# Key rope projection moved from two split-precision units to sixteen plain fp32 matmuls on four column tiles, with other work moved

## The chip, the cores and the metric

The kernel runs on one NeuronCore of one Trainium2 chip. The metric is the device time of one execution in microseconds (us), lower is better. TensorE (PE) does the matmuls, VectorE (DVE) and ScalarE (ACT) the elementwise work, GpSimd (POOL) and SyncE (SP) small jobs and the issue of DMAs.

## The reference, cut to what matters

One layer of a hybrid attention block, all in fp32, over 256 prompt tokens and 64 sample tokens (T = 320 token columns together). What the change touches is the MLA branch:

```python
h = rmsnorm(x, norm_pre[l])
proj = jnp.einsum('bsd,de->bse', h, w_in[l])          # D = 2048 in, 15392 out
a_qkv, b_qkv, c_qkv, d_in, gate_in, merge_in = jnp.split(proj, SPLIT_POINTS, axis=-1)
q_down, kv_down, k_rope_in = jnp.split(d_in, (Q_LORA, Q_LORA + KV_LORA), axis=-1)   # 384, 128, 32
q_mla = jnp.einsum('bsr,re->bse', rmsnorm(q_down, mla_q_norm[l]), mla_w_q_up[l])
ckv = rmsnorm(kv_down, mla_kv_norm[l])
k_rope = rope(k_rope_in, pos)                          # 32 columns
kv = jnp.einsum('bkr,re->bke', ckv_all, mla_w_kv_up[l])
```

The other parts are three attention branches (A stick-breaking, B banded, C differential), gates, branch and merge projections, the output projection and a last norm.

## The kernel before, in words

**Units.** The weights stream through the chip once, cut into units of at most 128x1024 elements. Each unit is loaded by SP (`emit_load`, L156, four buffers `raw`), split into a rounded high half on ACT (L193, `whi`) and the low rest on DVE (L194, `wlo`), and multiplied on PE. An fp32 product is made of three fast matmuls (`mm3`, L197 to L200: high x high, high x low, low x high), each 128x128 weights by 320 columns. A usual unit holds 256 output columns for four slices of the input, 24 matmuls; four such units (j = 0 to 3) make one group, which adds up in one of two PSUM buffers, `pm0` and `pm1`, that groups take in turn (`new_pm`, L102). After its last unit the group's `post` reads the buffer out; the buffer can be written again only when all of these reads are done. The input x is split once in the same way (`xhi`, `xlo`; first eight units).

**Slots.** The main loop (L1243 to L1267) runs one slot per unit i. In slot i it emits, in this order: the load for unit i+3, the split of unit i+3, a step of the background work (`run_background`, L283), the unit's matmuls, and its `post`. `whi` and `wlo` have four buffers, so the split of unit i+3 can start only when PE has finished unit i-1. Every engine runs its instructions in the order in which they were emitted (the schedule is written by hand).

**Order of the units.** Before: 0 to 7 the latent projections of branch D (`d_units`, L902; 512 columns, in two `pm` buffers); 8 and 9 the key rope (`krope_units`, L788); 10 to 13 the first A query; 14 `kv_unit(0)` (L826); 15 to 18 A key; 19 `kv_unit(1)`; 20 `q_unit(0)` (L855); 21 to 24 A value; 25 `q_unit(1)`; 26 to 29 a gate; 30 `q_unit(2)`; then groups of four to the end of the first phase, then merges and branches, then the output projection.

**Key rope.** Its 32 columns and a copy of them with the halves swapped are one weight of 64 columns. The split puts the high and the low half side by side (`pack`, L180 to L186), so one 128-column weight serves both, and two matmuls per input slice (L799, L800) give the product: 32 matmuls in all. `post` adds the two halves, scales and rotates.

**Work around it.** `x_rms` (L1198) sums the squares of x on PE, ahead of unit 7; the squares come from a chain of adds on DVE (`x_sum`, L1196). `x_rbc` (L1208), ahead of unit 8, spreads the norm over all partitions. The post of units 0 to 7 runs in slot 8 and starts `kv_norm` and `q_norm` (L746, L773) as background work: `q_norm` first steps in slot 9, waits 3 slots, sums on PE in slot 12, waits 4 slots, and in slot 16 makes three transposes on PE (L585), three scalings on DVE (L783), the high half `qh` on ACT (L785) and the low half `ql` on DVE (L786), which the `q_unit`s multiply by.

**kv_unit and q_unit.** `kv_unit` takes a `pm` buffer for the keys and two of the four small `att` PSUM buffers for the values (18 matmuls), and reads the `pm` buffer out with two copies on DVE (L847) and two on ACT (L848), the values with L843, L849 and L850, and copies the rope keys in with L852. `q_unit(0)` has 18 matmuls and six DVE operations behind them (L875 to L880).

**Attention in the background.** `pair` (L248) steps the attention of two head pairs at a time. Scores of the first go into the PSUM buffer that the running group does not use (`spare_pm`, L106). A `yield n, True` is a place where both wait until such a buffer may be taken: `spare_ok` (L245) allows it in the second and third unit of a group (j = 1 and 2).

**Start.** SP loads the first slice of x, ACT's queue the first weights. Meanwhile PE multiplies a tile of ones seven times (`spin`, L130).

Of the kernel before, what the change touches and what calls it, by code (L numbers as in the profile page):

```python
# [29 lines left out]
NCP = 128  # L30
# [30 lines left out]
def hybrid_streaming_kernel(ctx, tc, ins, outs):  # L61
# [48 lines left out]
    def att():  # L110
        return psa.tile([128, 512], F32, name="att", tag="att", bufs=4)
# [6 lines left out]
    ident = cpool.tile([128, NCP], F32, name="ident")  # L118
# [3 lines left out]
    def load_x(a, b):  # L122
        nc.sync.dma_start(xf[:, a:b, :], ins["x_t"][:, a:b, :])
# [6 lines left out]
    spin = att()  # L130
    for _ in range(7):
        nc.tensor.matmul(spin[:, 0:128], ones, ones, start=True, stop=True)
# [7 lines left out]
    def rb(n, i=0, rows=slice(0, 128), cols=slice(0, T)):  # L140
        w = cols.stop - cols.start
        r = rbc[rows, i:i + 1, cols]
        return r if n == 1 else r.to_broadcast([rows.stop - rows.start, n, w])
# [15 lines left out]
    def load_part(q, u, k0, k1, c0=0, c1=None):  # L159
# [5 lines left out]
        q.dma_start(raw[:, k0:k1, c0:c1], src[:, k0:k1, c0:c1])  # L165
# [10 lines left out]
    def emit_split(u):  # L176
        n = u["kn"] * u["cols"]
        hi = wpool.tile([128, 1024], F32R, name="whi", tag="whi", bufs=NHL)
        raw = u["raw"][:, :n]
        if u.get("pack"):  # L180
            hl = hi.rearrange("p (k o c) -> p k o c", o=2, c=u["cols"])
            raw = raw.rearrange("p (k c) -> p k c", c=u["cols"])
            nc.scalar.activation(hl[:, :, 0, :], raw, AF.Copy)
            nc.vector.tensor_tensor(hl[:, :, 1, :], raw, hl[:, :, 0, :].bitcast(F32), op=OP.subtract)
            u["hi"] = hi
            return  # L186
# [58 lines left out]
    def spare_ok():  # L245
        return slot[0] >= len(units) or units[slot[0]].get("left", 0) > 0

    def pair(*gens):  # L248


        live = [dict(gen=g, due=0, bar=None) for g in gens]
        while live:
            go = True
            while go:
# [10 lines left out]
                if live and all(e["bar"] and e["due"] <= slot[0] for e in live):  # L265
                    if live[0]["bar"][1] and not spare_ok():
# [201 lines left out]
    def attn_softmax(kind, n, hf, p, q, k, v, bias_heads=None):  # L468
# [13 lines left out]
        yield 0, True  # L482
# [17 lines left out]
        yield 0, False  # L500
# [19 lines left out]
        if kind != "C":  # L520
            for c, (a, b) in enumerate(BLK):
                nc.vector.tensor_scalar(z[:, a:b], z[:, a:b], rs[:, c:c + 1], None, op0=OP.mult)
            yield 2, True
            zt = transposes_pt(z, p)
            yield 2, False
# [12 lines left out]
        yield 3, False  # L538
# [9 lines left out]
        yield 2, False  # L548
# [10 lines left out]
        yield 2, False  # L559
# [28 lines left out]
    def attn_stick(n, hf, p, q, k, v):  # L588
# [4 lines left out]
        yield 0, True  # L593
# [11 lines left out]
        yield 0, False  # L605
# [52 lines left out]
        yield 2, False  # L658
# [73 lines left out]
    def post_d1(ps):  # L732
# [4 lines left out]
        scaled(M["kvd"][:, 0:1, :], ps[:, 1:2, :T], 1)  # L737
        scaled(M["qd"][:, 2:3, :], ps[:, 0:1, :T], 1)
# [49 lines left out]
    def krope_units():  # L788
        box = {}

        def mk(j):
            def mm(u):
                if j == 0:
                    box["ps"] = att()[:, :T]
                h = u["hi"].rearrange("p (k c) -> p k c", c=128)
                ps = box["ps"]
                for kk in range(8):
                    k = 8 * j + kk
                    nc.tensor.matmul(ps, h[:, kk, :], xhi[:, k, :], start=k == 0, stop=False)  # L799
                    nc.tensor.matmul(ps, h[:, kk, :], xlo[:, k, :], start=False, stop=k == 15)  # L800
            return mm

        def post():

            p1, ps, ce, kr = R["p1"], box["ps"], R["ce"], M["kr"]
            ka = p1.tile([96, 2, T], F32, name="ka", tag="t0", bufs=2)
            nc.scalar.activation(ka[0:64, 0, :], ps[64:128, :], AF.Copy)
            nc.vector.tensor_tensor(ka[0:64, 0, :], ka[0:64, 0, :], ps[0:64, :], op=OP.add)
            nc.vector.tensor_tensor(ka[0:64, 0, :], ka[0:64, 0, :], rbc[0:64, 0, :], op=OP.mult)
            nc.vector.tensor_tensor(kr[64:96, 0:T], ka[0:32, 0, :], ce[0:32, C_CS:C_CS + T], op=OP.mult)  # L810
            nc.vector.tensor_tensor(ka[64:96, 1, :], ka[32:64, 0, :], ce[32:64, C_CS:C_CS + T], op=OP.mult)
            nc.vector.tensor_tensor(kr[64:96, 0:T], kr[64:96, 0:T], ka[64:96, 1, :], op=OP.add)
            kz = p1.tile([128, 2, 448], F32, name="kz", tag="t2", bufs=2)
            M["kz"] = kz
            nc.gpsimd.memset(kz[64:128], 0.0)
            for j in range(2):
                for o in range(2):
                    a = 64 + 32 * o + 16 * j
                    nc.gpsimd.dma_start(kz[a:a + 16, j, :], kr[64 + 16 * o:80 + 16 * o, :])
            defer(lambda: nc.sync.dma_start(O["o_krope_t"], kr[64:96, 0:T]))  # L820

        for j in range(2):
            units.append(dict(src=w_kr[j * 1024:(j + 1) * 1024, :], kn=8, cols=64, mm=mk(j),
                              post=post if j == 1 else None, pack=True))
# [77 lines left out]
    def d_units():  # L902
# [4 lines left out]
        def mk(j):  # L907
            def mm(u):
                if j == 0:
                    box.extend(new_pm() for _ in range(2))  # L910
                h, l = (u[n].rearrange("p (k c) -> p k c", c=512) for n in ("hi", "lo"))
                for kk in range(2):
                    k = 2 * j + kk
                    wx = ((h, xhi), (h, xlo), (l, xhi))
# [293 lines left out]
    def x_rbc():  # L1208
        tp = att()
        for t, n in TN:  # L1210
            nc.tensor.transpose(tp[:, t * 128:t * 128 + n], rstat[:n, 2 * t:2 * t + 1].to_broadcast([n, 128]), ident[:n, :n])
        nc.scalar.activation(rbc[:, 0, :], tp[:, :T], AF.Copy)
        nc.vector.tensor_scalar(rbc[:, 1, :], tp[:, :T], 0.125, None, op0=OP.mult)
# [10 lines left out]
             6: [lambda: x_sum(0, 2, 2), lambda: x_sum(0, 1, 1)]}  # L1224
    late = {7: x_rms, 8: x_rbc}
# [17 lines left out]
    for i, u in enumerate(units):  # L1243
# [83 lines left out]
```

## Time and profile before

| what | value |
|---|---|
| median of 3 runs | 1178.18 us (1177.75 to 1178.98) |
| the profiled execution's own time | 1178.78 us |
| its span, first to last instruction | 1176.9 us |
| PE busy | 1166.2 us (99%) |
| DVE, ACT, POOL busy | 611.0, 507.2, 62.2 us (52%, 43%, 5%) |
| DMA | 182.94 MB, mean 155 GB/s |
| mean granted TensorE clock | 0.999 |

Busy time is that in which an engine works on at least one instruction. Matmuls overlap in the pipeline, so one that is shown with 0.31 us can follow the one ahead of it by 0.147 us; the distance between starts is what counts. A plain fp32 matmul appears as two records, one for each of its two passes.

### The profile page before, as it was taken

How to read it: one execution, taken by the hardware profiler on the slowest of the kernel's cores; microseconds unless marked ns; L12 is line 12 of the kernel's file. 1: busy time of each engine (PE TensorE's matmuls, PEld its weight loads, DVE VectorE, ACT ScalarE, POOL GpSimd, SP SyncE). 2: the span in 40 equal slices, each digit the busy share in tenths (PEclk: the TensorE clock that was granted, in tenths of full speed). 3: DMA queues.
4: the chain of work that ended last, by engine and by line, in shares of the span. 5: the costliest groups of instructions: out<-in, count | busy, mean ns of one | idle time of the engine just before them, and what ended most of it. 6: DMA issues, size and time to landing. Idle time of an engine off the chain costs nothing.

```text
span 1176.9 us, 19581 instructions
## 1 busy us (share of the span) xinstructions
PE 1166.2 (99%) x8135; PEld 1154.3 (98%) x8135; DVE 611.0 (52%) x853; ACT 507.2 (43%) x732; POOL 62.2 (5%) x124
## 2 busy tenths in 40 slices
PE   9999999999999999999999999999999999999997
PEld 9999999999999999999999999999999999999997
DVE  7583547455664547547445454454444454454444
ACT  8444664347445546535333333333333333334442
POOL 0312000002022100000000000000000000020000
PEclk9999999999999999999999999999999999999999
DMA  8866435545455544455554555555555555565442
GB/s 271 245 193 186 131 113 162 155 145 149 148 163 142 160 143 137 126 160 145 148 157 141 154 145 151 155 150 144 158 147 144 161 144 148 157 201 180 144 125 90
DMA packets 173449, 182.94 MB, mean 155 GB/s; under 512 B 9197, under 2 KB 167265, under 8 KB 172945
## 3 DMA queue, kind: packets, MB, share of 16 engines
q1 hardware_dynamic: 169488, 173.20, 50.1%
q0 software_dynamic: 2656, 5.32, 1.7%
q10 hardware_dynamic: 1216, 3.18, 0.9%
q8 instruction: 64, 1.05, 0.4%
q14 instruction: 25, 0.20, 0.1%
HBM read 174.79 MB, written 9.39 MB: 156 GB/s over the span
## 4 chain that ended last, share of the span: by engine, by line
PE 96%; ACT 1%; DMA 1%; DVE 1%; issue 0%; SPq 0%; DVEq 0%
PE pm L198 30%; PE pm L200 29%; PE pm L199 29%; PE att L411 1%; DMA raw<-in_w_in 1%; PE pm L1116 0%; PE pm L1118 0%; PE pm L1117 0%; ACT xhi L1185 0%; ACT whi L171 0%; PE pm L921 0%; PE att L648 0%; PE sp L498 0%; PE att L1081 0%; DVE xsq L1196 0%
## 5 line engine op out<-in xcount | busy, mean ns | idle before, releaser
L194 DVE TENSOR_TENSOR wlo<-raw,whi 128x1024 fp32r<-128x1024 f32 (+1 forms) x301 | 366.3, 1222 | 456.3 <-ACT whi L193 454.6
L198 PE MATMUL pm<-xhi,whi 128*128 128x320 f32 x1856 | 577.1, 311 | 0.0
L200 PE MATMUL pm<-xhi,wlo 128*128 128x320 f32 x1856 | 573.5, 309 | 0.0
L199 PE MATMUL pm<-xlo,whi 128*128 128x320 f32 x1856 | 573.5, 309 | 0.0
L193 ACT ACTIVATE whi<-raw 128x1024 fp32r<-128x1024 f32 (+1 forms) x301 | 315.1, 1052 | 411.3 <-PE pm L199 329.7
L198 PEld LDWEIGHTS pm<-xhi,whi 128*128 128x128 f32 x1856 | 348.4, 188 | 1.8 <-PE att L200 0.6
L199 PEld LDWEIGHTS pm<-xlo,whi 128*128 128x128 f32 x1856 | 348.5, 188 | 0.2
L200 PEld LDWEIGHTS pm<-xhi,wlo 128*128 128x128 f32 x1856 | 348.4, 188 | 0.0
L198 PE MATMUL pm<-ghi,whi 128*128 128x320 f32 x256 | 79.1, 309 | 0.0
L199 PE MATMUL pm<-glo,whi 128*128 128x320 f32 x256 | 79.1, 309 | 0.0
L200 PE MATMUL pm<-ghi,wlo 128*128 128x320 f32 x256 | 79.1, 309 | 0.0
L970 ACT ACTIVATE sg<-sg 128x640 f32<-128x640 f32 x32 | 23.7, 741 | 111.3 <-DVE sg L147 111.3
L198 PE MATMUL pm<-yhi,whi 128*128 128x320 f32 x224 | 69.7, 311 | 0.0
L199 PE MATMUL pm<-ylo,whi 128*128 128x320 f32 x224 | 69.2, 309 | 0.0
L200 PE MATMUL pm<-yhi,wlo 128*128 128x320 f32 x224 | 69.2, 309 | 0.0
L147 DVE TENSOR_TENSOR sg<-pm,rbc 128x640 f32<-128x640 f32 x40 | 33.0, 824 | 44.6 <-PE pm L200 44.6
L198 PEld LDWEIGHTS pm<-ghi,whi 128*128 128x128 f32 x256 | 48.0, 188 | 0.0
L199 PEld LDWEIGHTS pm<-glo,whi 128*128 128x128 f32 x256 | 48.0, 188 | 0.0
L200 PEld LDWEIGHTS pm<-ghi,wlo 128*128 128x128 f32 x256 | 48.0, 188 | 0.0
L199 PEld LDWEIGHTS pm<-ylo,whi 128*128 128x128 f32 x224 | 42.1, 188 | 0.0
L198 PEld LDWEIGHTS pm<-yhi,whi 128*128 128x128 f32 x224 | 42.1, 188 | 0.0
L200 PEld LDWEIGHTS pm<-yhi,wlo 128*128 128x128 f32 x224 | 42.0, 188 | 0.0
(330 smaller groups left out, 892.8 us busy)
## 6 DMA issues: line engine op xcount, KB each, us to landing
raw<-in_w_in SPq DMA_DIRECT2D x237, 512.0 KB, 3.8
raw<-in_w_branch SPq DMA_DIRECT2D x32, 512.0 KB, 3.6
raw<-in_w_out SPq DMA_DIRECT2D x32, 512.0 KB, 3.7
xrp<-in_x_prompt SPq DMA_DIRECT2D x1, 2048.0 KB, 7.7
out_xp<-ytp SPq DMA_DIRECT2D x8, 256.0 KB, 2.1
xf<-in_x_t SPq DMA_DIRECT2D x5, 321.0 KB, 7.5
scr<-in_bb ACTq DMA_DIRECT2D x1, 1536.0 KB, 8.9
bp<-scr POOLq DMA_DIRECT2D x12, 128.0 KB, 2.4
```

The lines of the kernel that those rows point to most:

```text
L147: nc.vector.tensor_tensor(out, ps, rb(n, i, rows, cols), op=OP.mult)
L193: nc.scalar.activation(h, raw, AF.Copy)
L194: nc.vector.tensor_tensor(l, raw, h.bitcast(F32), op=OP.subtract)
L198: nc.tensor.matmul(out, wh, xh, start=first, stop=False)
L199: nc.tensor.matmul(out, wh, xl, start=False, stop=False)
L200: nc.tensor.matmul(out, wl, xh, start=False, stop=last)
L411: nc.tensor.matmul(o[64 * j:64 * j + 64, a:b], v[:, blk, vc + 64 * j:vc + 64 * j + 64], z[j][blk], start=first, stop=not first)
L970: nc.scalar.activation(s, s, AF.Sigmoid)
```

## The change

- The key rope's two units go. Its weight (128 x 16 x 32) is loaded once by SP into its own tile `wkr` behind the identity, and multiplied by `norm_pre` on DVE in slot 6 (`kr_scale`). Sixteen plain fp32 matmuls of 32 output columns each, from the unsplit x (`krope_mm`, behind unit 7), add up on four column tiles of the array: slice k on tile k mod 4. In slot 9 ACT copies the result to SBUF, and in slot 10 one fp32 matmul with a constant of 64 columns (`sel`) adds the four tiles and makes the swapped copy; the rotation follows as before (`krope`).
- `x_rms` is emitted inside unit 7, between its two input slices, instead of ahead of it. Its PSUM tile serves `x_rbc` too.
- The D units use one `pm` buffer and two `att` buffers, instead of two `pm` buffers.
- Order of the units after: 0 to 7 D; 8 to 11 A query; 12 to 15 A key; 16 `kv_unit(0)`; 17 `kv_unit(1)`; 18 `q_unit(0)`; 19 to 22 A value; 23 `q_unit(1)`; 24 to 27 a gate; 28 `q_unit(2)`. The slots of `q_norm` stay 9, 12 and 16.
- The places at which scores take the spare buffer allow only j = 2 now; those for transposes still j = 1 and 2.
- The first loads of x and of the weights are halved by partitions over SP's and ACT's queues; `spin` runs eight times, in a spare `pm` buffer.

```diff
-    def spare_ok():
-        return slot[0] >= len(units) or units[slot[0]].get("left", 0) > 0
+    def spare_ok(most):
+        return slot[0] >= len(units) or 0 < units[slot[0]].get("left", 0) <= most
...
-    spin = att()
-    for _ in range(7):
+    spin = spare_pm()[:, 0]
+    for _ in range(8):
...
-        yield 0, True
+        yield 0, 1
...
-            yield 2, True
+            yield 2, 2
...
+    def krope_mm():
+
+        M["krp"] = att()
+        for k in range(KC):
+            c = slice(32 * (k % 4), 32 * (k % 4) + 32)
+            nc.tensor.matmul(M["krp"][c, :T], wkr[:, k, :], xf[:, k, :T], start=k < 4, stop=k >= KC - 4)
+
+    def krope():
+        p1, ce, kr = R["p1"], R["ce"], M["kr"]
+        ka = p1.tile([128, 2, T], F32, name="ka", tag="t0", bufs=2)
+        nc.scalar.activation(ka[:, 0, :], M["krp"][:, :T], AF.Copy)
+        yield 1
+
+        ps = att()[:, :T]
+        nc.tensor.matmul(ps[0:64], sel, ka[:, 0, :], start=True, stop=True)
+        nc.vector.tensor_tensor(ka[0:64, 1, :], ps[0:64], rbc[0:64, 0, :], op=OP.mult)
...
                 if j == 0:
-                    box.extend(new_pm() for _ in range(2))
+                    box.append(new_pm())
+                    box.append([att(), att()])
...
+                    if k == KC - 1:
+                        x_rms()
...
+                if j == 7:
+                    krope_mm()
...
     d_units()
-    krope_units()
...
     aq()
+    ak()
     kv_unit(0)
-    ak()
     kv_unit(1)
     q_unit(0)
...
-    load_part(nc.scalar, units[0], 0, 1, 0, 256)
-    load_x(0, 1)
-    load_part(nc.scalar, units[0], 0, 1, 256, 512)
+    for q, r in ((nc.sync, slice(0, 64)), (nc.scalar, slice(64, 128))):
+        load_x(0, 1, q, r)
+        load_part(q, units[0], 0, 1, 0, 256, r)
+    load_part(nc.sync, units[0], 0, 1, 256, 512)
...
+    def kr_scale():
+        nc.vector.tensor_tensor(wkr, wkr, xf[:, :, T:T + 1].to_broadcast([128, KC, 32]), op=OP.mult)
...
-             6: [lambda: x_sum(0, 2, 2), lambda: x_sum(0, 1, 1)]}
-    late = {7: x_rms, 8: x_rbc}
+             6: [lambda: x_sum(0, 2, 2), lambda: x_sum(0, 1, 1), kr_scale]}
+    late = {8: x_rbc}
...
-                nc.sync.dma_start(ident, ins["cp"])
+                nc.sync.dma_start(cp, ins["cp"])
+                nc.sync.dma_start(wkr, ins["w_kr"])
                 nc.sync.dma_start(nrm, ins["nrm"])
```

## Rows read from the trace of the kernel before

**Rows 1.** The page: busy time by engine; the chain by engine.

```profile
PE 1166.2 (99%) x8135; PEld 1154.3 (98%) x8135; DVE 611.0 (52%) x853; ACT 507.2 (43%) x732; POOL 62.2 (5%) x124
...
PE 96%; ACT 1%; DMA 1%; DVE 1%; issue 0%; SPq 0%; DVEq 0%
```

**Rows 2.** Waits of PE, whole span: us in total, times, longest.

```profile
PE sp L498 <- DVE sg L147: 1.6, 1, 1.6
PE att L1202 <- DVE xsq L1196: 1.1, 1, 1.1
...
```

**Rows 3.** Timeline, PE, 30 to 42 us: start, us, what, idle before.

```profile
30.45 0.31 PE L921 MATMUL pm<-xhi,wlo 128*128 128x320 f32 x1
31.84 0.81 PE L1202 MATMUL att<-ones,xsq 128*128 128x2 f32 x6 [1.08 <-DVE xsq L1196]
32.58 0.41 PE L921 MATMUL pm<-xhi,whi 128*128 128x320 f32 x1
...
36.71 0.42 PE L799 MATMUL att<-xhi,whi 128*128 128x320 f32 x1
...
41.50 0.72 PE L576 MATMUL att<-ones,kvd 128*128 128x2 f32 x6
```

**Rows 4.** Timeline, DVE, 29 to 32 us.

```profile
29.83 0.69 DVE L184 TENSOR_TENSOR whi<-raw,whi 128x512 fp32r<-128x512 f32 x1
30.43 1.35 DVE L1196 TENSOR_TENSOR xsq<-xsq 128x640 f32<-128x640 f32 x2
```

**Rows 5.** Timeline, DVE, second attention of C: 450 to 458 us.

```profile
453.26 0.82 DVE L147 TENSOR_TENSOR sg<-pm,rbc 128x640 f32<-128x640 f32 x1
...
457.57 0.35 DVE L397 CUSTOM_DVE_ANT_0 z<-sp,bs 128x192 f32<-128x192 f32 x1
```

**Rows 6.** Timeline, PE, 0 to 8 us.

```profile
1.04 3.35 PE L132 MATMUL att<-ones 128*128 128x128 f32 x14 [1.04 <-POOL ones L129]
4.76 0.90 PE L921 MATMUL pm<-xhi,whi 128*128 128x320 f32 x2 [0.36 <-ACT whi L171]
```

**Rows 7.** Chain that ended last, its longest pieces: start, us, what.

```profile
148.28 1.92 PE att L411 x32
...
440.94 1.08 PE att L567 x4
```

**Rows 8.** L411 in all: duration ns min/median/max, first and last start, forms.

```profile
L411 PE MATMUL att<-zt,v x128: 219/247/431, 148.2 to 395.4; 128*64 128x64 f32 x64, 128*64 128x256 f32 x32, 128*64 128x128 f32 x32
```

**Rows 9.** Timeline, DVE, slot 16: 67 to 73 us.

```profile
68.07 1.45 DVE L783 SCALAR_TENSOR_TENSOR qd<-qd,smallp,att 128x320 f32<-128x320 f32 x3
70.59 1.16 DVE L786 TENSOR_TENSOR ql<-qd,qh 128x960 fp32r<-128x960 f32 x1 [1.07 <-ACT qh L785]
71.66 0.95 DVE L194 TENSOR_TENSOR wlo<-raw,whi 128x768 fp32r<-128x768 f32 x1
```

**Rows 10.** Timeline, PE, transposes of slot 16; starts of units 19, 20, 21.

```profile
64.33 0.49 PE L585 MATMUL att<-ident,rs 128*128 128x128 f32 x3
64.58 0.39 PE L198 MATMUL pm<-xhi,whi 128*128 128x320 f32 x1
...
75.22 0.36 PE L198 MATMUL pm<-ch,whi 128*128 128x448 f32 x1
...
77.86 0.31 PE L198 MATMUL pm<-qh,whi 128*128 128x320 f32 x1
...
80.49 0.31 PE L198 MATMUL pm<-xhi,whi 128*128 128x320 f32 x1
```

**Rows 11.** Timeline, DVE, slot 19: 75 to 82 us.

```profile
75.42 0.82 DVE L147 TENSOR_TENSOR k<-pm,rbc 128x640 f32<-128x640 f32 x1 [1.30 <-PE pm L200]
76.42 1.22 DVE L194 TENSOR_TENSOR wlo<-raw,whi 128x1024 fp32r<-128x1024 f32 x1 [0.17 <-ACT whi L193]
77.56 0.61 DVE L847 COPY kd<-pm 64x448 f32<-64x448 f32 x1
78.78 0.62 DVE L847 COPY kd<-pm 64x448 f32<-64x448 f32 x1 [0.61 <-ACT kd L848]
...
81.26 1.23 DVE L194 TENSOR_TENSOR wlo<-raw,whi 128x1024 fp32r<-128x1024 f32 x1
```

**Rows 12.** Timeline, ACT, slot 19: the last read of the buffer.

```profile
79.43 0.54 ACT L848 ACTIVATE kd<-pm 64x448 f32<-64x448 f32 x1 [0.68 <-DVE kd L847]
```

More of the change, by code (lines that the diff above doesn't have):

```diff
@@ L28 @@
 LAM_INIT = 0.8 - 0.6 * math.exp(-0.0)
-NCP = 128
+NCP = 192
 C_TRI, C_MD, C_MS, C_CS, C_OH = 0, 128, 384, 512, 832
@@ L37, in make_consts @@
     cp[:, 0:128] = np.eye(128)
+    r = np.arange(128) % 32
+    cp[np.arange(128), 128 + r] = cp[np.arange(128), 160 + (r + 16) % 32] = 1.0
     ce = np.zeros((128, NCE), np.float32)
@@ L117, in hybrid_streaming_kernel, with load_x @@
     xsq = ppool.tile([128, KC, T], F32, name="xsq")
-    ident = cpool.tile([128, NCP], F32, name="ident")
+    cp = cpool.tile([128, NCP], F32, name="cp")
+    ident, sel = cp[:, 0:128], cp[:, 128:192]
+    wkr = ppool.tile([128, KC, 32], F32, name="wkr")
     nrm = cpool.tile([128, 24], F32, name="nrm")
     npost = nrm[:, 0:16]
-    def load_x(a, b):
-        nc.sync.dma_start(xf[:, a:b, :], ins["x_t"][:, a:b, :])
+    def load_x(a, b, q=nc.sync, r=slice(0, 128)):
+        q.dma_start(xf[r, a:b, :], ins["x_t"][r, a:b, :])
     eps = cpool.tile([128, 1], F32, name="eps")
@@ L142, in rb @@
         r = rbc[rows, i:i + 1, cols]
-        return r if n == 1 else r.to_broadcast([rows.stop - rows.start, n, w])
+        return r[:, 0] if n == 1 else r.to_broadcast([rows.stop - rows.start, n, w])
     def scaled(out, ps, n, i=0, rows=slice(0, 128), cols=slice(0, T)):
@@ L157, in emit_load, with load_part @@
         load_part(nc.sync, u, 0, u["kn"])
-    def load_part(q, u, k0, k1, c0=0, c1=None):
+    def load_part(q, u, k0, k1, c0=0, c1=None, r=slice(0, 128)):
         kn, c = u["kn"], u["cols"]
@@ L164, in load_part @@
         src = u["src"].rearrange("(k p) c -> p k c", p=128)
-        q.dma_start(raw[:, k0:k1, c0:c1], src[:, k0:k1, c0:c1])
+        q.dma_start(raw[r, k0:k1, c0:c1], src[r, k0:k1, c0:c1])
     def hi_part(u, a, b):
@@ L179, in emit_split @@
         raw = u["raw"][:, :n]
[L180 to L186, printed above, removed]
         lo = wpool.tile([128, 1024], F32R, name="wlo", tag="wlo", bufs=NHL)
@@ L265, in pair @@
                 if live and all(e["bar"] and e["due"] <= slot[0] for e in live):
-                    if live[0]["bar"][1] and not spare_ok():
+                    if live[0]["bar"][1] and not spare_ok(live[0]["bar"][1]):
                         break
@@ L499, in attn_softmax @@
             scale = 1.0
-        yield 0, False
+        yield 0, 0
         if p == 0:
@@ L537, in attn_softmax @@
         nc.vector.tensor_scalar(z[:, 768:960], z[:, 768:960], st[:, 15:16], None, op0=OP.mult)
-        yield 3, False
+        yield 3, 0
         zt = p1.tile([128, 1024], F32, name="zt", tag="t1", bufs=2)
@@ L547, in attn_softmax @@
         copy_on(1, zt[:, 768:1024], tp[:, 0:256])
-        yield 2, False
+        yield 2, 0
         o = att()
@@ L558, in attn_softmax @@
         nc.scalar.activation(oc[:, 1, :], oc[:, 0, :], AF.Square)
-        yield 2, False
+        yield 2, 0
         rnorm(oc[:, 1, :], oc[:, 1, :], 128)
@@ L592, in attn_stick @@
         t2 = p1.tile([128, 1024], F32, name="a2", tag="t2", bufs=2)
-        yield 0, True
+        yield 0, 1
         if p == 0:
@@ L604, in attn_stick @@
                 nc.tensor.matmul(S[j][:, a:b], k[r, p, kb:kb + 128], q[r, p, kb:256], start=True, stop=True)
-        yield 0, False
+        yield 0, 0
         if p:
@@ L657, in attn_stick @@
         mask(t1)
-        yield 2, False
+        yield 2, 0
         both = t1[:, 0:512].rearrange("p (b j c) -> p j b c", b=2, j=2)
@@ L736, in post_d1 @@
         M["kvd"] = p1.tile([128, 3, T], F32, name="kvd", tag="t1", bufs=2)
-        scaled(M["kvd"][:, 0:1, :], ps[:, 1:2, :T], 1)
-        scaled(M["qd"][:, 2:3, :], ps[:, 0:1, :T], 1)
+        scaled(M["kvd"][:, 0, :], ps[1][:, :T], 1)
+        scaled(M["qd"][:, 2, :], ps[0][:, :T], 1)
         nc.scalar.activation(M["kvd"][:, 1, :], M["kvd"][:, 0, :], AF.Square)
@@ L786, in q_norm @@
         nc.vector.tensor_tensor(M["ql"], qd, M["qh"].bitcast(F32), op=OP.subtract)
[L788 to L820, printed above, removed]
@@ new lines, in krope_mm @@
+    def krope_mm():
[11 more added lines that the diff above has]
+        nc.vector.tensor_tensor(ka[0:64, 1, :], ps[0:64], rbc[0:64, 0, :], op=OP.mult)
+        nc.vector.tensor_tensor(kr[64:96, 0:T], ka[0:32, 1, :], ce[0:32, C_CS:C_CS + T], op=OP.mult)
+        nc.vector.tensor_tensor(ka[64:96, 0, :], ka[32:64, 1, :], ce[32:64, C_CS:C_CS + T], op=OP.mult)
+        nc.vector.tensor_tensor(kr[64:96, 0:T], kr[64:96, 0:T], ka[64:96, 0, :], op=OP.add)
+        kz = p1.tile([128, 2, 448], F32, name="kz", tag="t2", bufs=2)
+        M["kz"] = kz
+        nc.gpsimd.memset(kz[64:128], 0.0)
@@ L822, in krope_units @@
         for j in range(2):
-            units.append(dict(src=w_kr[j * 1024:(j + 1) * 1024, :], kn=8, cols=64, mm=mk(j),
-                              post=post if j == 1 else None, pack=True))
+            for o in range(2):
+                a = 64 + 32 * o + 16 * j
+                nc.gpsimd.dma_start(kz[a:a + 16, j, :], kr[64 + 16 * o:80 + 16 * o, :])
+        defer(lambda: nc.sync.dma_start(O["o_krope_t"], kr[64:96, 0:T]))
     def kv_unit(hf):
@@ L920, in mm @@
                         w, x = wx[i]
-                        nc.tensor.matmul(box[m // 2][:, m % 2, :T], w[:, kk, m * 128:(m + 1) * 128], x[:, k, :],
+                        nc.tensor.matmul((box[0][:, m] if m < 2 else box[1][m - 2])[:, :T], w[:, kk, m * 128:(m + 1) * 128], x[:, k, :],
                                          start=k == 0 and i == 0, stop=k == KC - 1 and i == 2)
+                if j == 7:
+                    krope_mm()
             return mm
@@ L927, in post @@
             post_d0(box[0])
+            light.append(krope())
         for j in range(8):
@@ L1196, in x_sum @@
         nc.vector.tensor_tensor(xsq[:, a:a + n, :], xsq[:, a:a + n, :], xsq[:, c:c + n, :], op=OP.add)
+    def kr_scale():
+        nc.vector.tensor_tensor(wkr, wkr, xf[:, :, T:T + 1].to_broadcast([128, KC, 32]), op=OP.mult)
     def x_rms():
         acc = xsq[:, 0, :]
-        ps = att()
+        ps = M["rms"] = att()
         for t, n in TN:
@@ L1208, in x_rbc @@
     def x_rbc():
-        tp = att()
+        tp = M["rms"][:, 64:64 + T]
         for t, n in TN:
             nc.tensor.transpose(tp[:, t * 128:t * 128 + n], rstat[:n, 2 * t:2 * t + 1].to_broadcast([n, 128]), ident[:n, :n])
-        nc.scalar.activation(rbc[:, 0, :], tp[:, :T], AF.Copy)
-        nc.vector.tensor_scalar(rbc[:, 1, :], tp[:, :T], 0.125, None, op0=OP.mult)
+        nc.scalar.activation(rbc[:, 0, :], tp, AF.Copy)
+        nc.vector.tensor_scalar(rbc[:, 1, :], tp, 0.125, None, op0=OP.mult)
         ppool_ctx.close()
@@ L1301 @@
     kr = np.asarray(inputs["w_in"])[0, :, COL_D + 512:COL_D + 544]
-    arrays["w_kr"] = np.ascontiguousarray(np.concatenate([kr, kr[:, 16:32], kr[:, 0:16]], axis=1))
+    arrays["w_kr"] = np.ascontiguousarray(kr.reshape(KC, 128, 32).transpose(1, 0, 2))
     arrays["cp"], arrays["ce"], arrays["cq"] = make_consts()
```

2 lines of the change are left out of this document (1 added, 1 removed).

## The prediction

> **What bounds the kernel now.** I read the page first. PE is busy for 99% of the span, and the chain that ended last is 96% PE [rows 1]. So time is won or lost only where PE issues fewer or longer matmuls, or where it stands idle. Next the list of PE's waits. After its first instruction it holds two of more than half a microsecond, 1.6 us for a spare buffer and 1.1 us for the sum of squares [rows 2]; DVE and ACT, at half load, are late for PE nowhere else. Then the timelines of PE at the places that the change touches, and there those of DVE and ACT, since the order on these two queues decides when a PSUM buffer comes free. In a steady stretch a 320-column matmul takes 0.1465 us from start to start (the 18 of `q_unit(0)` 2.63 us, 77.86 to 80.49 [rows 10]), a usual unit of 24 so 3.52.
>
> **What is removed.** The rope's 32 matmuls run from 36.71 to 41.50 [rows 3]: 4.79 us. About 0.1 of it is the first one's later follow-up after the small tiles of `x_rbc`, which unit 8 will pay instead: 4.7.
>
> The sum of squares: the last matmul of unit 6 starts at 30.45, so `x_rms` could start at 30.60; it starts at 31.84, when DVE's last adds are done [rows 3, 4]. 1.24 us idle. Moved behind twelve matmuls of unit 7 it is due at 30.60 + 12 x 0.147 = 32.36. DVE is later then too: the split of unit 8 that stands ahead of these adds is now a full one of 1.14 (76.42 to 77.56 [rows 11]) in place of the rope's 0.60 (29.83 to 30.43 [rows 4]), so the sum is ready at 31.84 + 0.54 = 32.38. The wait is met by chance to within 0.1: gain 1.2 (bounds 0.6 and 1.24). `kr_scale` is emitted behind the adds, so it delays the splits of units 9 and 10 and the reciprocals only, which have over 2 us: unit 7's second half and the rope stand ahead of `x_rbc`.
>
> The spare buffer: the second attention of C waited until DVE had read out a gate, at 453.26 + 0.82 = 454.08 [rows 2, 5]. By the code it now takes its buffer at j = 2. I counted the slots of all pairs through both orders: from the second pair on they start 1 to 5 slots later against the groups, the work ends 5 slots later, still 5 ahead of the phase's end. At this place the norm of the first C attention, which filled DVE, lies three slots ahead of the scores as before, but its group's read-out comes directly behind it in DVE's order, without a split between. Gain 1.6 (bounds 0 and 1.6). The price of j = 2 is that the next group wants the buffer two units later, 7 us, not three; the scores' last read comes at 457.57 + 0.35, 3.8 us behind the buffer's grant [rows 5]. That is hidden, with 3 us to spare; if not, the excess is PE's wait.
>
> The start: fourteen records of `spin` end 3.35 us behind 1.04, and the first real matmul starts at 4.76, after 0.36 us idle [rows 6]. Two more records at 0.21 to 0.24 each hold PE to about 4.6 to 4.8, so however early the halved loads land, no more than 0.15 is won; a slice of x that now needs both queues may land later. I take 0.1 (bounds -0.3 and 0.3). PE's first matmuls are slow (two records in 0.90 [rows 6]), at the lower level of its clock, 1.2 GHz; no row says what would move its rise, and I count nothing for it.
>
> Sum of the gains: 4.7 + 1.2 + 1.6 + 0.1 = 7.6 us.
>
> **What is added on PE.** A plain fp32 matmul of 320 columns costs two passes of 0.27 (four records in 1.08 [rows 7]). No row shows tiles of 32 columns; the nearest are the 64-column tiles of L411. One such stretch has 32 records in 1.92 us [rows 7]; from the forms [rows 8], a quarter of all, it streams 8 x 256 + 8 x 128 + 16 x 64 = 4096 columns. At 0.27 per 320 that would be 3.46 us one by one and 1.73 two abreast. So two run abreast, and 0.2 is the change of tile shape there and back. I take four abreast for four tiles: 16 matmuls in 4 rounds of 2 passes, 8 x 0.27 = 2.16, plus 0.25 for the shape: 2.4. Bounds: 2.4, and 32 x 0.27 + 0.25 = 8.9 if they run one by one. `sel` is one matmul, 0.54 + 0.25 = 0.8.
>
> The Trainium skill (TensorE: Matmul & The Clock Gate, Part 3: Packing small matmuls — row/col tiling) measured three column tiles of 32 at 2.38 times one, not 3; at the same share of the ideal the rounds would take 2.7 us by an estimate from that page, half a microsecond over mine. The 64-column rows here come out nearer to the ideal.
>
> **What is moved: the kv units.** Here I expect a loss. `q_norm`'s last step stays in slot 16. Before, that was a unit of A's key, with four more units to come before `q_unit(0)`. Now slot 16 is `kv_unit(0)`, and `q_unit(0)` is two units later and needs the PSUM buffer of `kv_unit(0)`. Behind the end of unit 15 (time 0), DVE's order is: read-out of A's key, low split of unit 19, `q_norm`, the copies out of `kv_unit(0)`, low split of unit 20, the copies out of `kv_unit(1)`.
>
> - As in slot 19 of before (75.22 [rows 10] to 77.56 [rows 11]) the first two end at 2.34.
> - `q_norm` takes 68.07 to 71.66 [rows 9], with DVE's wait for `qh` in it: 3.59, so 5.93. ACT's copies can't pass either: `qh` is ahead of them.
> - The copies go in turn DVE, ACT, DVE, ACT: 77.56 to 79.43 + 0.54 [rows 11, 12], 2.41. The buffer is free at 8.34.
> - PE: transposes 64.33 to 64.58 and 0.1 of follow-up, 0.35 [rows 10]; two kv units of 2.64 (75.22 to 77.86): at 5.63 it wants the buffer. **Wait 2.7.** `q_unit(0)` runs from 8.4 to 11.0 (2.63, 77.86 to 80.49).
> - DVE comes to the split of unit 20 3.70 behind its first copy (77.56 to 81.26), at 9.63, ends it 1.14 later, and the second copies take 2.41: `kv_unit(1)`'s buffer is free at 13.2. A's value wants it at 11.0. **Wait 2.2.**
>
> Behind the waiting matmuls stands all of PE's work, so both count in full: 4.9. A's value units (14 us) then let DVE catch up: unit 21 needs its low split at 20 and gets it at about 16. In before no copy was late: A's value started at 80.49, 0.5 behind the buffer's end. Bounds 0 and 6.
>
> **Hidden.** The 256 KB of `wkr` go on SP's queue behind unit 7's load, in place of 512 KB of rope units that go; `kr_scale` reads them 15 us later. ACT loses two 512-wide packs and gains one 320-wide copy. The store of the rope result moves behind unit 15's load in SP's order, which frees that load. Rope keys for L852 are wanted six slots after `krope`. `kv_unit(0)`'s load and POOL's memset of its values move with it, behind A's key on SP and behind the bias DMAs of slot 15 on POOL; the load has three slots, and the values are first read after slot 29. If any cover is gone, the unit at hand waits by the excess.
>
> **The sum.** Added 2.4 + 0.8 + 4.9 = 8.1, removed 7.6: 0.5 us longer. The profiled execution's own time of 1178.78 (1.9 us around its span, which stay) becomes 1179.3; it lies 0.6 above the median of 1178.18, so the forecast for the median is **1178.7**. About 0.2%, 2.4 us, is what a measurement of this kernel can tell from no change: this is none.
>
> **The rivals.**
> 1. *The kv waits don't come* (copies pass `q_norm`, or its step finds DVE earlier). For it: the waits of before hold none of this kind, and DVE is half idle. Against: DVE's rows of slots 14 to 19 stand in emitted order throughout. Then 1178.7 - 4.9 = 1173.8. With only the first wait 1176.5.
> 2. *The four tiles don't run abreast.* Place: behind unit 7, where nothing hides it. One by one 6.5 more, 1185.2; two abreast 2.2 more, 1180.9. It decides, that is makes the kernel slower by over 0.2%, once the sixteen matmuls cost 4.3 instead of 2.4. For it: two abreast is all that a row shows; against: those two pay nothing for each other.
> 3. *The later scores meet new waits*, in attention or at the start: gain of 1.7 lost and as much again, about 1182.
>
> **Chances.** Forecast as worked out 0.58 (own range 1176.8 to 1180.5), rival 1 in full 0.16, in part 0.06, rival 2 0.11, rival 3 0.09. Faster by over 0.2% (below 1175.8): 0.20, rival 1 and some of its partial form. Slower (above 1180.5): 0.22, rivals 2 and 3 and the forecast's upper edge. Within: 0.58. The range 1173.4 to 1182.2 leaves out the tiles one by one and the tails.
>
> **What would show it.** In the profile after: waits of PE on DVE or ACT copies of kd (L847, L848 of before) of 2 to 3 us each, ahead of `q_unit(0)` and A's value; rope matmuls in 2.2 to 2.5 us with four starts within a few hundredths; `x_rms` with a wait under 0.2; no wait of scores for a gate; A's query starting near 38 us, where before the rope still ran. The prediction falls with the kv waits, by 5 us downward, or with the tiles, by 2 to 6 upward.

## The result, and the profile after

| | before | after |
|---|---|---|
| median | 1178.45 us (4 runs, three of them those of the table above) | 1183.86 us (4 runs, 1183.72 to 1186.25) |
| ratio to before, 95% interval | | 1.0051 [1.0038, 1.0064] |
| the profiled execution's own time, its span | 1178.78, 1176.9 us | 1183.72, 1181.9 us |

The kernel became slower by half a per cent; 1178.7 was forecast, with 1182.2 as the upper end. The page of the kernel after, busy time by engine and the chain by engine:

```profile
PE 1167.3 (99%) x8139; PEld 1151.9 (97%) x8139; DVE 610.8 (52%) x851; ACT 509.1 (43%) x732; POOL 61.3 (5%) x124
...
PE 95%; DVE 1%; ACT 1%; DMA 1%; issue 0%; SPq 0%; DVEq 0%; ACTq 0%
```

PE is still the bound [rows 1], and its busy time is 1.1 us more, though the rope takes 1.8 us less of it (4.79 before, 2.29 and 0.68 after): something made its work slower too. The waits of PE after:

```profile
PE pm L195 <- ACT kd L836: 4.6, 2, 2.7
PE sp L136 <- POOL ones L133: 1.0, 1, 1.0
PE att L646 <- DVE ll L640: 0.9, 1, 0.9
PE att L1199 <- DVE xsq L1190: 0.8, 1, 0.8
PE pm L912 <- DVE wlo L178: 0.2, 1, 0.2
```

Beside [rows 2]: the wait of the scores for the spare buffer is gone, two waits for the copies out of the kv units have come, the running sums of an A pair have a new one (L646), and the sum of squares keeps most of its own. PE's rows of what was added, and the squares' additions on DVE:

```profile
33.33 0.81 PE L1199 MATMUL att<-ones,xsq 128*128 128x2 f32 x6 [0.77 <-DVE xsq L1190]
...
36.04 2.36 PE L791 MATMUL att<-xf,wkr 128*32 128x320 f32 x32
38.33 0.63 PE L1208 MATMUL att<-cp,rstat 128*128 128x128 f32 x3
...
46.69 0.75 PE L800 MATMUL att<-ka,cp 128*64 128x320 f32 x2
47.37 0.41 PE L195 MATMUL pm<-xhi,whi 128*128 128x320 f32 x1
```

```profile
22.32 1.49 DVE L1190 TENSOR_TENSOR xsq<-xsq 128x1280 f32<-128x1280 f32 x1 [0.20 <-ACT xsq L1186]
...
30.80 1.22 DVE L191 TENSOR_TENSOR wlo<-raw,whi 128x1024 fp32r<-128x1024 f32 x1
31.93 1.34 DVE L1190 TENSOR_TENSOR xsq<-xsq 128x640 f32<-128x640 f32 x2
```

The rope is as cheap as forecast: 2.29 us from its first start to that of `x_rbc` behind it (36.04 to 38.33), and 0.68 us for `sel` (46.69 to 47.37). The last additions begin at 31.93; before it was 30.43 [rows 4]. They are late from the first addition on, 22.32, which in before was:

```profile
21.36 1.49 DVE L1196 TENSOR_TENSOR xsq<-xsq 128x1280 f32<-128x1280 f32 x1 [0.20 <-ACT xsq L1192]
```

The kv waits, on DVE, ACT and PE, in order of time:

```profile
72.85 1.46 DVE L781 SCALAR_TENSOR_TENSOR qd<-qd,smallp,att 128x320 f32<-128x320 f32 x3
...
75.45 1.16 DVE L784 TENSOR_TENSOR ql<-qd,qh 128x960 fp32r<-128x960 f32 x1 [1.14 <-ACT qh L783]
...
76.00 0.28 PE L197 MATMUL att<-whi,cl 128*64 128x256 f32 x1
76.53 0.61 DVE L835 COPY kd<-pm 64x448 f32<-64x448 f32 x1
...
78.39 0.54 ACT L836 ACTIVATE kd<-pm 64x448 f32<-64x448 f32 x1 [0.68 <-DVE kd L835]
...
78.99 0.41 PE L195 MATMUL pm<-qh,whi 128*128 128x320 f32 x1 [2.71 <-ACT kd L836]
...
83.24 0.54 ACT L836 ACTIVATE kd<-pm 64x448 f32<-64x448 f32 x1 [0.68 <-DVE kd L835]
...
83.83 0.41 PE L195 MATMUL pm<-xhi,whi 128*128 128x320 f32 x1 [1.94 <-ACT kd L836]
```

PE starts its last matmul of the second kv unit at 76.00, but the first copy out of the first one only starts at 76.53, when the query norm's step (72.85 to 76.6) lets DVE go. From start to start the gaps are 2.99 us ahead of `q_unit(0)` and 2.25 ahead of A's value; less the steps of 0.12 and 0.15 us at the same places in before, 5.0 us is lost.

What no step foresaw comes right behind. PE by stretches of 1 us: length, busy time and records, granted clock, DMA share, GB/s:

```profile
83.00:84.00 1.00, 0.17 (x1) 1.00 0.99 337
84.00:85.00 1.00, 1.00 (x6) 0.69 0.37 127
85.00:86.00 1.00, 1.00 (x6) 0.50 0.00 0
86.00:87.00 1.00, 1.00 (x5) 0.50 0.00 0
87.00:88.00 1.00, 1.00 (x6) 0.61 0.53 96
88.00:89.00 1.00, 1.00 (x9) 1.00 1.05 358
```

After the second gap the granted clock falls to half, from 2.4 to 1.2 GHz, for some 3 us, and 320-column matmuls stand 0.267 us apart instead of 0.147. Nothing waits there, so no list of waits shows it.

The last new wait, DVE and PE in one timeline:

```profile
191.24 1.18 DVE L151 TENSOR_TENSOR q<-pm,rbc 128x512 f32<-128x512 f32 x3
192.46 1.23 DVE L191 TENSOR_TENSOR wlo<-raw,whi 128x1024 fp32r<-128x1024 f32 x1
...
193.03 0.40 PE L646 MATMUL att<-lh,trr 128*128 128x512 f32 x1
...
193.60 1.29 DVE L640 TENSOR_TENSOR ll<-a,lh 128x512 fp32r<-128x512 f32 x2
...
194.34 0.50 PE L646 MATMUL att<-ll,trr 128*128 128x512 f32 x1 [0.91 <-DVE ll L640]
```

PE comes to the low half of the running sums when DVE has just begun it, behind a query's read-out and a weight split.

Starts of matmuls cut a profiled execution into five stretches: to A's first query product; on to the first product with low weights of A's value; on to the 32nd such product (84.23 to 99.41 after); on to the last matmul (1174.72 after); and what lies around. The forecast's row is before's plus its terms; the kv norm's sums (0.66) lie ahead of the first cut in before and behind it in all others but e3.

| kernel | to A's query | to A's value | A's value | to the last | around | own time |
|---|---|---|---|---|---|---|
| before | 42.09 | 38.69 | 13.64 | 1075.64 | 8.72 | 1178.78 |
| forecast | 37.83 | 45.05 | 13.64 | 1074.04 | 8.72 | 1179.28 |
| after | 38.89 | 45.34 | 15.17 | 1075.32 | 9.00 | 1183.72 |
| e1 | 39.06 | 42.00 | 13.64 | 1075.30 | 9.06 | 1179.06 |
| e2 | 39.83 | 45.35 | 13.64 | 1075.32 | 9.00 | 1183.14 |
| e3 | 41.50 | 40.54 | 13.64 | 1075.60 | 8.60 | 1179.88 |
| e4 | 42.78 | 45.34 | 13.64 | 1075.32 | 9.02 | 1186.10 |
| e5 | 39.83 | 40.09 | 13.64 | 1074.02 | 8.98 | 1176.56 |
| e6 | 38.30 | 40.09 | 13.64 | 1075.34 | 8.75 | 1176.12 |
| e7 | 39.55 | 40.09 | 13.64 | 1075.31 | 9.05 | 1177.64 |
| e8 | 37.96 | 40.09 | 13.64 | 1075.33 | 9.03 | 1176.05 |
| e9 | 37.37 | 40.09 | 13.64 | 1074.01 | 8.56 | 1173.67 |
| e10 | 39.70 | 45.33 | 13.64 | 1075.30 | 9.03 | 1183.00 |
| e11 | 39.26 | 45.34 | 15.17 | 1075.30 | 9.02 | 1184.09 |

After against the forecast, by columns: +1.06, +0.29, +1.53, +1.28, +0.28, in sum 4.44 us. One execution of the same code also differs from the next in the first column: it is 42.09 and 41.50 in before and e3, which are alike up to there, and 38.89 to 39.83 in after, e1, e2, e10 and e11. The medians, with ratios to before on the same chip:

| kernel | median us | ratio | 95% |
|---|---|---|---|
| e1 query norm's step in slot 14 | 1179.46 | 1.0005 | 0.9996 to 1.0014 |
| e2 both waits filled | 1183.06 | 1.0035 | 1.0023 to 1.0047 |
| e3 before, with the new order alone | 1181.06 | 1.0018 | 1.0009 to 1.0027 |
| e4 rope tile after tile | 1187.48 | 1.0073 | 1.0060 to 1.0085 |
| e7 kv units apart | 1177.65 | 0.9989 | 0.9980 to 0.9998 |
| e5 = e7, A pairs' old rule | 1176.44 | 0.9981 | 0.9972 to 0.9990 |
| e6 = e7, old start | 1175.24 | 0.9973 | 0.9962 to 0.9983 |
| e8 = e7, norm's sums behind unit 7 | 1176.25 | 0.9981 | 0.9972 to 0.9989 |
| e9 = e7 with e5, e6 and e8 | 1173.82 | 0.9958 | 0.9946 to 0.9971 |
| e10 only the first wait filled | 1184.88 | 1.0050 | 1.0036 to 1.0065 |
| e11 the changed kernel again | 1184.93 | 1.0052 | 1.0040 to 1.0065 |

### The profile page after: what moved, and what is told of

Same layout as the page of the kernel before. It is cut to its first block, busy times and chain, and to the rows that moved or that the text cites. A ratio compares the mean times of both kernels' runs of the same rounds, so it can differ in the third digit from the quotient of the medians.

```text
span 1181.9 us, 19600 instructions
## 1 busy us (share of the span) xinstructions
PE 1167.3 (99%) x8139; PEld 1151.9 (97%) x8139; DVE 610.8 (52%) x851; ACT 509.1 (43%) x732; POOL 61.3 (5%) x124
## 4 chain that ended last, share of the span: by engine, by line
PE 95%; DVE 1%; ACT 1%; DMA 1%; issue 0%; SPq 0%; DVEq 0%; ACTq 0%
PE pm L195 29%; PE pm L197 29%; PE pm L196 29%; PE att L409 1%; DMA raw<-in_w_in 1%; PE pm L1109 0%; PE pm L1111 0%; PE pm L1110 0%; DVE wlo L191 0%; ACT xhi L1179 0%; PE att L646 0%; ACT whi L175 0%; PE sp L496 0%; PE att L1074 0%; DVE xsq L1190 0%
```

## The experiments

**The kv waits.** Theory: the query norm's step stands on DVE ahead of the copies that free the buffers. Rival: two units of one product each right behind a key group are too close, whatever DVE does.

e1, on the changed kernel, in `q_norm`:

```diff
         rs = rnorm_front(sq[:, 0, :], 384)
-        yield 4
+        yield 2
```

> The changed kernel, with VectorE's step of the query norm (the three scaled products, the copy and the subtraction) issued two slots earlier, in slot 14 instead of 16. Theory: the waits of 2.99 and 2.25 us ahead of q0 and of A's value (4.87 us over the usual gap) are there because that step stands on VectorE ahead of the additions that free the PSUM buffers, and the fall of the granted clock at 84.4 us follows from them. Then the first wait is gone (0 to 0.3), the second is at most 1.3 us, the clock stays at 1.00 there, and the time is 1178 to 1179.5 us. Rival: the buffers are too close whatever stands on VectorE (two units of one product each right behind a key group), and the waits stay above 3.5 us in sum: 1182.5 us or more. Second rival: the waits go but the clock falls elsewhere: 1179.5 to 1181.

Measured: 1179.46 us. The first wait is gone, one gap of 1.88 us stands ahead of A's value (a wait of 1.6 for the copies in its list; at most 1.3 was expected), the clock holds, and A's value takes 13.64. Two slots of one step of the norm are worth 4.7 us in the profiled executions (1183.72 to 1179.06), the clock's 1.53 included.

e3, on the kernel before:

```diff
     aq()
-    kv_unit(0)
     ak()
+    kv_unit(0)
     kv_unit(1)
```

> The kernel before, with one part of the change alone: A's key group goes ahead of both kv units (aq, ak, kv0, kv1, q0). The rope units stay, so that the query norm's step is two slots further behind A's query. Theory: it is the step's place on VectorE, not the order of the units, that makes the long waits: the first wait is 0 to 0.3, the second at most 2 us, and the time 1178 to 1180.5 us. Rival: the order alone makes both waits, 4 us or more together: 1182 us or more.

Measured: no first wait and a second gap of 1.88, as the theory has it, and 1179.88 in the profiled execution; but the median is 1181.06, half a microsecond above the stated range. Its eleven executions have a mean granted clock of 0.998 or 0.999 at 1179.86 to 1181.06 us, and of 0.997 in the five at 1181.62 to 1182.20. What makes these five slower is not shown: the kernel before, which has no such gap, also has nine of 28 executions on the same chip at 1179.94 to 1180.88 us, with 0.997 or 0.998. So the order alone costs one short wait; for the long ones the norm's step must also stand in `kv_unit(0)`'s own slot (16 after; in e3 the step is in slot 16 too, but `kv_unit(0)` in slot 18).

e7, on the changed kernel:

```diff
     aq()
-    ak()
     kv_unit(0)
+    ak()
     kv_unit(1)
...
         rs = rnorm_front(kvd[:, 1, :], 128)
-        yield 2
+        yield 1
...
         rs = rnorm_front(sq[:, 0, :], 384)
-        yield 4
+        yield 3
```

> The changed kernel, with A's key group back between the kv units (aq, kv0, ak, kv1, q0), the kv norm's step one slot earlier (11) and the query norm's one slot earlier (15). Theory: with four units of the key group between the two kv units, each takes its PSUM buffer from copies that are long done; both waits are at most 0.5 us together, the clock does not fall, and the time is 1176.5 to 1178.5 us, below the changed kernel by 5.5 to 7. Rival: the new wait only moves (kv0 right behind A's query meets the additions of that group, or the step in slot 15 meets the key group's): one wait of 1.5 to 3 us, 1179 to 1182 us.

Measured: 1177.65 us, within the theory's range, faster than before by 0.11% (interval 0.02 to 0.20). From A's query to A's value it takes 40.09 us, 5.25 less than after: the two gaps' 5.0, and the slower first matmuls behind each (0.25 instead of 0.15 us to the next start). Its waits of PE:

```profile
PE sp L136 <- POOL ones L133: 1.0, 1, 1.0
PE att L646 <- DVE ll L640: 0.9, 1, 0.9
PE pm L912 <- ACT whi L175: 0.8, 1, 0.8
PE att L1199 <- DVE xsq L1190: 0.8, 1, 0.8
PE pm L912 <- DVE wlo L178: 0.2, 1, 0.2
```

**The clock.** Theory: the waits make it fall. Rival: something else at that place does.

e2, on the changed kernel (the products of ones are extra work that nothing reads):

```diff
+    def filler(n):
+        f = att()
+        for _ in range(n):
+            nc.tensor.matmul(f[:, 0:128], ones, ones, start=True, stop=True)
...
+            if u0 == 0:
+                filler(11)
             ps = new_pm()
...
+                if j == 0 and slot[0] == 19:
+                    filler(9)
                 if j == 0:
                     box["ps"] = new_pm()
```

> The changed kernel, with 11 products of the tile of ones ahead of q0 and 9 ahead of A's value, into a buffer that nothing reads, so that TensorE works through most of the two waits; nothing else is moved. They are extra work, and should hide in the waits. Theory: the fall of the granted clock to 0.57 of its rate in 84 to 88 us is caused by the idle time of the two waits; with TensorE busy in them the clock stays at 1.00, the first products behind the waits start within 0.5 us of where they did, and the time is 1.3 to 2.3 us less than the changed kernel's, 1181.6 to 1182.6 us. Rival: the fall has another cause; then the clock falls as before, and the time is the same or up to 1 us more, 1183.5 to 1185.

PE of e2 by stretches, columns as above:

```profile
80.00:84.00 4.00, 4.00 (x30) 1.00 0.44 125
84.00:88.00 4.00, 4.00 (x30) 1.00 0.33 113
```

From A's query to A's value it is 45.35 us, as in the changed kernel (45.34): the waits are as long, only full. The clock stays at 1.00, and A's value takes 13.64 instead of 15.17. The 1.53 us are the idle time's. The median, 1183.06, missed its range: in the profiled execution the start took 0.94 us more than in that of after (39.83 against 38.89), which hides most of it. By the ratios to before on the same chip (1.0035 against 1.0051 and, in e11, 1.0052) e2 is 1.9 us better, with intervals that overlap.

e10 is e2 without the second filler, so with the 2.25 us idle:

```diff
-                if j == 0 and slot[0] == 19:
-                    filler(9)
```

> The changed kernel, with only the first of the two waits filled with products of the tile of ones (11 ahead of q0); the second stays idle. It asks whether one wait is enough for the clock to fall: e1 and e3, with a single gap of 1.88 us at the place of the second, kept 1.00. Theory: the fall needs both; with 2.25 us of the second alone the clock stays at 1.00 and the stretch from A's first value product to the 33rd low one takes 13.64 us, as in e2: 1182 to 1183.2 us. Rival: the second alone does it, and the stretch takes 15.17 us, as in the changed kernel: 1183.5 to 1184.5.

Measured: in the profiled execution the clock holds and A's value takes 13.64. But the median is 1184.88: two executions at 1182.67 and 1183.00 have a mean clock of 0.999, three at 1184.88 to 1186.26 have 0.996. In e2 the six are at 0.997 to 0.999. So the traced execution fits the theory, the median missed both ranges, and whether the second gap alone takes the clock down in some executions stays open: no trace shows where the three lost their time. That one gap can be enough, the first, e4 below shows in a trace.

e11, the changed kernel unaltered:

> The changed kernel unaltered, for more runs of it on the chip of the two others: how far its start and its clock vary from one execution to the next. Theory: the waits ahead of q0 and of A's value are 2.99 and 2.25 us again, the clock falls at the second again, unit 1 starts anywhere between 9.3 and 10.2 us: 1183 to 1185 us. Rival: the fall of the clock was that one execution's, and the median of more runs is near 1182.

Measured: 1184.93 us (1184.09 to 1186.67), mean clocks 0.995 to 0.997, the same gaps of 2.99 and 2.25 and again 15.17 for A's value. The fall is in both traces of this kernel. The mean clock is no measure of its cost: the traced execution of e11 has 0.996, that of after 0.998, with the same 15.17. They differ at the end of the span, behind the last matmul (1174.72 after, 1175.06 in e11), where the clock falls again and nothing is left for PE. PE by stretches in after and in e11:

```profile
1180.00:1181.00 1.00, 0.00 (x0) 0.53 0.02 8
```

```profile
1177.00:1178.00 1.00, 0.00 (x0) 0.62 0.00 0
```

**The four tiles.** e4, on the changed kernel, the same 16 products in another order:

```diff
-        for k in range(KC):
+        for k in sorted(range(KC), key=lambda k: k % 4):
             c = slice(32 * (k % 4), 32 * (k % 4) + 32)
```

> The changed kernel, with its 32 rope products in another order: the eight of one tile of 32 columns one behind the other, then those of the next tile. The products and their number are the same. Theory: the 2.29 us come from products on different tiles going abreast; eight in a row on one tile cannot, and the 32 take 32 x 0.27 = 8.6 us: the time is 1189 to 1191.5 us. Rival: a product on a quarter of the columns is cheap by itself, and the order is nothing: 1183.5 to 1185 us.

Rope records of e4 by stretches of 1 us (PE busy and records, weight loads, clock, DMA); a record that overlaps two stretches counts in both:

```profile
36.60:37.60 1.00, 0.98 (x4) 0.47 (x5) 1.00 0.68 154
37.60:38.60 1.00, 1.00 (x10) 0.45 (x8) 1.00 0.98 338
38.60:39.60 1.00, 1.00 (x10) 0.49 (x8) 1.00 0.80 198
...
41.60:42.60 1.00, 0.69 (x3) 0.10 (x1) 1.00 0.69 232
```

Measured: 1187.48 us, between the two expectations; the rope takes 5.59 instead of 2.29. The first four records start 0.27 apart, one at a time; then they come in pairs, and the last four are single again: 20 rounds of 0.27 instead of 8. So a record costs 0.27 whatever its tile, and only other tiles go abreast; but, by this count, PE began the next tile's products while four of the tile before were left, so even this order has two abreast. Both numbers expected were wrong, 8.6 and 2.3; that the tiles go abreast is shown.

The same run shows the clock fall inside the first wait. PE of e4, stretches of 1 us:

```profile
81.00:82.00 1.00, 0.00 (x0) 1.00 1.09 383
82.00:83.00 1.00, 0.12 (x1) 0.70 1.10 357
83.00:84.00 1.00, 1.00 (x4) 0.50 1.09 346
```

The first wait of 2.99 us (79.89 to 82.88) was enough; in after a gap of the same length passed with the clock at 1.00 (76 to 80 us). The stretch at half clock lay under `q_unit(0)` here and cost nothing: the second gap shrank from 2.25 to 0.92, since A's value waits for DVE anyway (45.34 us again).

**The other two waits, and the start**, all on e7.

e5, in the A pairs alone, ahead of their first scores:

```diff
-        yield 0, 1
+        yield 0, 2
```

> The kernel of e7_kv_spread, with the old rule for the first scores of the A pairs alone: they may start one slot earlier in a group again (left at most 2 instead of 1). The C attentions keep the new rule. Theory: the wait of the running sums for their low half (1.31 us, 186.90 us in e7) comes from the new slots of the A pairs, and is gone; the wait for the spare buffer at the second C attention does not come back, since its own rule stays: 1175.9 to 1176.9 us, 0.8 to 1.7 below e7. Rival: the low half is late for another reason, and the wait stays or moves: within 0.4 us of e7, 1177.3 to 1178.

DVE and PE of e5 at the running sums:

```profile
182.06 1.28 DVE L640 TENSOR_TENSOR ll<-a,lh 128x512 fp32r<-128x512 f32 x2
183.27 1.18 DVE L151 TENSOR_TENSOR q<-pm,rbc 128x512 f32<-128x512 f32 x3
...
183.66 0.39 PE L646 MATMUL att<-lh,trr 128*128 128x512 f32 x1
...
183.89 0.39 PE L646 MATMUL att<-ll,trr 128*128 128x512 f32 x1
```

Measured: 1176.44 us. One slot earlier the low half stands ahead of the query's read-out, and the wait is gone. From A's value to the end it is 1074.02 against 1075.31 of e7, 1.29 less, and 1.62 less than before: the spare buffer's wait of 1.6 does not come back, so that is the whole gain of the rule where it was meant. The medians give about 1 us; in the profiled execution the norm's wait had grown (1.2 in the list).

e6, the old start:

```diff
-    for q, r in ((nc.sync, slice(0, 64)), (nc.scalar, slice(64, 128))):
-        load_x(0, 1, q, r)
-        load_part(q, units[0], 0, 1, 0, 256, r)
-    load_part(nc.sync, units[0], 0, 1, 256, 512)
+    load_part(nc.scalar, units[0], 0, 1, 0, 256)
+    load_x(0, 1)
+    load_part(nc.scalar, units[0], 0, 1, 256, 512)
...
-    for _ in range(8):
+    for _ in range(7):
```

> The kernel of e7_kv_spread, with the first loads and the seven warm products of the kernel before. Theory: the new split of the first loads over two queues lands the first weights later, in some runs more than in others (unit 1 starts at 9.39, 9.74, 10.08 and 10.12 us in the four profiles with it, at 9.47 in the one without), and through the additions of the squares it makes the wait of the norm's sums too; without it unit 1 starts at 9.4 to 9.6 and the wait shrinks from 1.09 to at most 0.5 us: 1176.2 to 1177.2 us. Rival: the start's loads vary as much by the old way, and the wait is one of VectorE's own work: within 0.4 us of e7.

Measured: 1175.24 us, a larger gain than expected. ACT's split of the second slice of x, in the kernel after and in e6:

```profile
5.72 0.56 ACT L1179 ACTIVATE xhi<-xf 128x320 fp32r<-128x320 f32 x1 [0.34 <-DMA xf<-in_x_t]
```

```profile
4.97 0.55 ACT L1178 ACTIVATE xhi<-xf 128x320 fp32r<-128x320 f32 x1
```

It starts 0.75 us earlier by the old way (5.05 before). SP now issues three loads ahead of the second slice where it issued one, at about 0.6 us each (0.75 to 2.61), and the second slice's own at 2.65; that this is the reason is argued, not tried. PE starts unit 2 at 12.70 to 12.99 us in the four profiles with the old loads and at 13.04 to 13.99 in the nine with the new; the gap ahead of the norm's sums falls from 1.09 to 0.61 (at most 0.5 was expected), and what lies around is 0.3 less. To A's query it takes 38.30, less than in any of the seven profiles that have the new loads and the same code up to there (38.89 to 39.83).

e8, the norm's sums behind unit 7:

```diff
-                    if k == KC - 1:
-                        x_rms()
...
                 if j == 7:
+                    x_rms()
                     krope_mm()
```

> The kernel of e7_kv_spread, with the norm's sums behind the last product of unit 7 instead of between its two halves. Theory: the wait of 1.09 us there is VectorE's additions ending 0.9 us after TensorE is ready; 1.76 us later they are done, and the rope products behind the sums hide the root and the reciprocal, which VectorE does at about 36.8 us in either place: the time is 0.7 to 1.1 below e7, 1176.5 to 1177. Rival: what the wait gave is taken back at the spread of the norm behind the rope products (it needs the reciprocal), or the roots hold up ScalarE's split of the weights: 1177.4 to 1178.4 us.

Measured: 1176.25 us, a little better than expected; the wait is gone from the list and nothing behind took it back.

e9, e7 with the three edits together:

> The kernel of e7_kv_spread with the three further edits together: the A pairs' old rule (e5), the old first loads (e6) and the norm's sums behind unit 7 (e8). Theory: the three waits are at different places and their gains add up: against e7 about 1.3 to 1.6 us for the low half, 0.9 to 2.4 for the start, and what the start leaves of the norm's wait, 0.47 (0.61 less the usual 0.14): 1172.5 to 1174.5 us, all main waits of TensorE gone but the one for the tile of ones. Rival: a new wait, at the start or at the spread of the norm, takes one of them back: 1175 to 1176.5.

Measured: 1173.82 us, within the theory's range, 0.42% under the kernel before (interval 0.29 to 0.54), the version that beats both. The whole list of PE's waits:

```profile
PE sp L136 <- POOL ones L133: 1.0, 1, 1.0
PE pm L910 <- ACT whi L175: 0.2, 1, 0.2
```

## Why the prediction was wrong

- **Right: the rope on PE.** 2.29 for 2.4 and 0.68 for 0.8. The step took four abreast, and the round is 0.27 in after and in e4. One by one the 32 records would be 32 x 0.27 = 8.6, so the ratio is 3.8. The Trainium skill (TensorE: Matmul & The Clock Gate, Part 3: Packing small matmuls — row/col tiling) states 2.38 for three tiles, from which 2.7 had been estimated; the trace does better, and the measurement decides.
- **Right: the kv waits.** 5.0 for 4.9 (2.87 for 2.7 and 2.10 for 2.2), for the stated reason (e1, e7). Rival 1 is out.
- **Wrong: "no row says what would move its rise, and I count nothing for it".** Said of the start, it stood for the whole kernel. PE's own waits took the clock down behind them, 1.53 us in the profiled executions (after and e11 against e2). The forecast had two long gaps on record and priced them by their length alone. The Trainium skill (TensorE: Matmul & The Clock Gate, Why this matters for your kernels) warns that idle between bursts of matmuls brings the lower clock back; the traces of after (0.50 at 85 to 87 us, behind the gaps) and e4 (0.70 at 82 to 83 us, in the gap) agree.
- **Wrong: "The spare buffer ... Gain 1.6".** The gain at the second C attention is there in full (e5: 1.62). But the step looked at the rule's effect at that one place; for the slots it had counted for all other pairs it asked nothing of DVE. There the A pair's low half fell behind a read-out and a split, and 1.3 was lost. Rival 3 named this, at 0.09.
- **Mis-sized: the sum of squares.** Gain 1.2 forecast, 0.31 came (a gap of 0.93 over the usual step is left of 1.24). DVE's last additions began 1.50 us later. The full split that the step counted is 0.54 of it; the other 0.96, for which the step had no term, was there at the first addition already (22.32 against 21.36). The new loads may be a part of it: with the old ones (e6) the gap is 0.61 instead of 1.09 in e7, but with the new ones it is anything from 0.66 (e1) to 1.52 (e5), so how large a part stays open.
- **Wrong in sign: the start.** +0.1 forecast. Undone on e7 it gives 1.9 us by the two ratios, 1.5 by the profiled executions, through unit 2's start, the norm's wait and what lies around.
- The terms so found are 1.53 of clock, 1.3 at the running sums, 0.9 at the squares, 0.3 around and some 0.3 in the first matmuls behind the kv waits: 4.3 of the 4.4 us by which after's profiled execution is off. The median lies 0.7 further, 5.2 off: the profiled execution of before lay 0.6 above the median, as the forecast had it, and that of after 0.1 below.

## What to carry to other kernels

Price a TensorE wait by its length and by the clock behind it: here gaps of 2.99 and 2.25 us took another 1.5 in both traces of the changed kernel, while with one gap of 2.25 (e10) or 1.88 (e1, e3) alone the traced clock held. Units may only be moved next to each other after a look at what stands on the read-out engine's queue between them; two slots of one norm step were worth 4.7 us. A scheduling rule that is tightened for one wait moves every pair that obeys it, so restrict it to the one that has the wait.

## What the runs showed of the hardware

- The granted clock can fall within a TensorE gap of 2.99 us (e4, 82 to 83 us), and here stays at half for some 3 us of full work; the cost depends on what is behind it, 1.53 us in A's value, nothing where a later wait absorbed it.
- The fall does not come at the same place: in after and e11 the clock held through the same gap of 2.99 us and fell within 1 us of the end of the next, of 2.25.
- The mean clock of an execution counts the idle end of its span too: 0.998 and 0.996 (after, e11) went with the same 1.53 us lost in A's value.
- Products on four column tiles of 32 start within 0.03 us of each other, and a badly ordered list still ran two tiles abreast.
